# Hand-overs between the sub-layers of a two-layer decoder step: earlier weight splits with a third buffer, moments summed in one accumulator each, and an eviction moved amid a post-norm

## The chip, the core and the metric

The kernel runs on one NeuronCore of one Trainium2 chip. The metric is the device time of one execution in microseconds (us). The engines are named as in the profile: PE is TensorE (PEld its weight loads), DVE is VectorE, ACT is ScalarE, POOL is GpSimd, SP is SyncE, which issues the DMAs. Each engine takes its own instructions in one fixed order.

## What is computed

One inference step of two layers on 512 prompt tokens and 8 x 8 sample tokens, 576 columns in all, model width 1024, in fp32. Each layer is FFN, token mixer, FFN; the mixer of layer 0 is a state-space layer with a gated output (S5 and GLU), that of layer 1 a latent attention (MLA). So there are six sub-layers, n = 0 to 5: FFN, S5, FFN, FFN, MLA, FFN. Every one is wrapped in two norms:

```python
def rms_norm(x, g):
    xf = x.astype(F32)
    y = xf * lax.rsqrt(jnp.mean(xf * xf, axis=-1, keepdims=True) + EPS)
    return (y * g.astype(F32)).astype(x.dtype)

def swiglu(x, w_gate, w_up, w_down):
    return (jax.nn.silu(x @ w_gate) * (x @ w_up)) @ w_down
...
h = swiglu(rms_norm(x, p['norm_pre'][i, 0]), p['ffn_w_gate'][i, 0], p['ffn_w_up'][i, 0], p['ffn_w_down'][i, 0])
x = x + 0.5 * rms_norm(h, p['norm_post'][i, 0])
```

## The kernel before

**Tiling.** Activations lie with the width on the 128 partitions (8 chunks) and the 576 columns in two halves of 288, half 0 and half 1. An fp32 product is made of three matmuls of rounded parts (`mm3`, lines 212 to 215): weight high by activation high, high by low, low by high. So every weight is split after its DMA: ACT copies the high part `whi` and DVE subtracts to the low part `wlo` (`load` in `big_pools`, lines 231 to 241, and `split`, 206 to 210), in pieces of 1024 columns, two for a full unit. The buffers `wlo` and `whi` have a number `nb` of turns: two in sub-layers 0 to 4, three from the output projection of MLA on (`open_w(2)` at line 879, `open_right()` at 1177). `XH` and `XL` (in the trace XHL) are the two parts of the pre-normed activations, `X` the residual, `Y` the output of a sub-layer.

**A hand-over.** The last two output blocks of a sub-layer, m = 6 and 7, run in `tail` (line 287). Their eviction adds to three accumulators over m by `ymom` (line 167): ACC (squares of Y), R (Y times X times gain) and ACQ (squares of Y times gain). For m below 7 the term goes through a buffer `sq` and POOL adds it (in MLA DVE adds ACQ); for m = 7 it stays in a tile of its own (`sqd`, `t`). `mom_a` (line 141) sums all six tiles over the partitions by small matmuls on PE (`sums`, line 100, line L106 of the trace), takes the inverse root of the ACC part on DVE (`rsqrt`, `diag`) and copies the R and ACQ part out (`rs_bc`, line 152). `spread` (line 184, L187) brings the result to all partitions, and `post` (line 274) runs `post1` for the eight chunks k: `t` on DVE (L265), the residual add to X on POOL or DVE (L267), and `xsplit`, the next sub-layer's high part on ACT and low part on DVE (L210). `mom_b` (line 155) forms the statistics of the next pre-norm from the moments, without reading X again.

In program order `tail` runs m = 6 and 7 of half 0, `mom_a` of half 0, m = 6 of half 1, the load and split of the next sub-layer's first weights (W0), all of `post` of half 0, then m = 7 of half 1. `mom_a` and `post` of half 1 are put off (`state["pend"]`) and run inside the next sub-layer's `first_units` (line 316), after its k = 0 and k = 2. `first_units` does two weight units at once: for each k, half 0 of both units, then half 1 unit by unit; the second unit's weights (W1) are loaded just before it (`loads`, line 283).

**What sets the order.** A planner orders the instructions of each engine: it runs the program on its own timing model and gives each engine, whenever that is free, the ready instruction that stands first in the program. Program order is thus a rank and no fixed order. `tc.issue_after(i)` puts what is written inside it behind instruction i on i's engine, and on that engine alone. Between S5 (n = 1) and the FFN before it the tail differs (`nxt == 1`): no split, and half 1's post-norm is spread over S5's own steps.

## Time and profile before

| | us |
|---|---|
| median of 3 runs | 2467.28 (2465.83 to 2472.31) |
| profiled execution | 2468.39 |
| its span, first to last instruction | 2466.6 |
| PE busy in it | 2392.4 (97%) |
| DVE busy | 1301.8 (53%) |
| ACT busy | 888.8 (36%) |
| POOL busy | 565.6 (23%) |

The busy times are unions over the whole span. A matmul's end is modelled, so a busy PE may still run at the lower of its two clocks; PEclk in the page and in the stretches is the granted clock as a share of 2.4 GHz. Idle time of an engine is written in brackets behind the instruction that ended it, with what released that instruction.

### The profile page before, as it was taken

How to read it: one execution, taken by the hardware profiler on the slowest of the kernel's cores; microseconds unless marked ns; L12 is line 12 of the kernel's file. 1: busy time of each engine (PE TensorE's matmuls, PEld its weight loads, DVE VectorE, ACT ScalarE, POOL GpSimd, SP SyncE). 2: the span in 40 equal slices, each digit the busy share in tenths (PEclk: the TensorE clock that was granted, in tenths of full speed). 3: DMA queues.
4: the chain of work that ended last, by engine and by line, in shares of the span. 5: the costliest groups of instructions: out<-in, count | busy, mean ns of one | idle time of the engine just before them, and what ended most of it. 6: DMA issues, size and time to landing. Idle time of an engine off the chain costs nothing. (4 is left out here: it accounts for less than half of the span.)

```text
span 2466.6 us, 44725 instructions
## 1 busy us (share of the span) xinstructions
PE 2392.4 (97%) x17814; PEld 2326.3 (94%) x17814; DVE 1301.8 (53%) x2807; ACT 888.8 (36%) x1864; POOL 565.6 (23%) x820
## 2 busy tenths in 40 slices
PE   7999999799999999999999999999999999999997
PEld 7999999779999999999999999898888899999997
DVE  7565666574564234456323444867777676323334
ACT  4222333374332222333222223424666543223221
POOL 3124455313421001152100115430000042100112
PEclk9999999899999999999999999999999989999999
DMA  3225434462222222122223222346555422222221
GB/s 127 86 76 159 139 127 123 130 178 90 69 86 81 71 98 86 65 82 74 82 73 98 78 79 76 117 123 188 172 166 168 140 78 77 76 87 87 86 71 63
DMA packets 114643, 254.92 MB, mean 103 GB/s; under 512 B 25121, under 2 KB 53538, under 8 KB 114178
## 3 DMA queue, kind: packets, MB, share of 16 engines
q1 hardware_dynamic: 114434, 252.06, 32.3%
q8 instruction: 140, 2.29, 0.4%
q14 instruction: 69, 0.57, 0.1%
HBM read 231.79 MB, written 22.59 MB: 103 GB/s over the span
## 5 line engine op out<-in xcount | busy, mean ns | idle before, releaser
L213 PE MATMUL ps<-XHL,whi 128*128 128x288 f32 x3344 | 997.9, 299 | 17.7 <-ACT whi L208 12.4
L214 PE MATMUL ps<-XHL,whi 128*128 128x288 f32 x3344 | 995.4, 298 | 4.5 <-DVE XHL L210 4.3
L215 PE MATMUL ps<-XHL,wlo 128*128 128x288 f32 x3344 | 988.7, 296 | 2.5 <-DVE wlo L208 2.5
L213 PEld LDWEIGHTS ps<-XHL,whi 128*128 128x128 f32 x3344 | 631.8, 189 | 21.7 <-ACT whi L208 12.8
L214 PEld LDWEIGHTS ps<-XHL,whi 128*128 128x128 f32 x3344 | 633.1, 189 | 8.7 <-DVE XHL L210 7.6
L215 PEld LDWEIGHTS ps<-XHL,wlo 128*128 128x128 f32 x3344 | 633.4, 190 | 3.7 <-DVE wlo L208 3.6
L208 DVE TENSOR_TENSOR wlo<-raw,whi 128x1024 fp32r<-128x1024 f32 (+2 forms) x349 | 410.0, 1199 | 268.1 <-ACT whi L208 267.6
L208 ACT ACTIVATE whi<-raw 128x1024 fp32r<-128x1024 f32 (+2 forms) x349 | 321.6, 946 | 428.8 <-PE ps L214 349.8
L213 PE MATMUL ps<-HH,whi 128*128 128x288 f32 x1408 | 418.8, 297 | 3.9 <-ACT whi L208 3.9
L215 PE MATMUL ps<-HH,wlo 128*128 128x288 f32 x1408 | 417.5, 297 | 1.4 <-DVE wlo L208 1.4
L214 PE MATMUL ps<-HL,whi 128*128 128x288 f32 x1408 | 418.0, 297 | 0.0
L371 POOL TENSOR_TENSOR t<-t,t 128x288 f32<-128x288 f32 x176 | 145.0, 824 | 1086.3 <-DVE t L370 972.4
L213 PEld LDWEIGHTS ps<-HH,whi 128*128 128x128 f32 x1408 | 266.6, 189 | 4.7 <-ACT whi L208 4.4
L215 PEld LDWEIGHTS ps<-HH,wlo 128*128 128x128 f32 x1408 | 266.7, 189 | 2.2 <-DVE wlo L208 2.2
L214 PEld LDWEIGHTS ps<-HL,whi 128*128 128x128 f32 x1408 | 266.8, 189 | 0.2
L370 DVE TENSOR_TENSOR t<-ps,R 128x288 f32<-128x288 f32 x176 | 80.2, 456 | 319.6 <-PE ps L215 319.5
L369 ACT ACTIVATE t<-t 128x288 f32<-128x288 f32 x176 | 77.9, 443 | 332.0 <-DVE t L368 315.8
L208 ACT ACTIVATE HH<-t 128x288 fp32r<-128x288 f32 x176 | 77.0, 438 | 242.4 <-POOL t L371 237.3
L178 POOL TENSOR_TENSOR ACC<-ACC,sq 128x288 f32<-128x288 f32 x72 | 82.4, 1144 | 314.7 <-ACT sq L176 314.7
L208 DVE TENSOR_TENSOR HL<-t,HH 128x288 fp32r<-128x288 f32 x176 | 80.6, 459 | 135.3 <-ACT HH L208 135.0
L368 DVE TENSOR_TENSOR t<-ps,R 128x288 f32<-128x288 f32 x176 | 79.3, 450 | 50.8 <-PE ps L215 50.7
L424 DVE TENSOR_TENSOR Y<-ps,Y 128x288 f32<-128x288 f32 x64 | 29.2, 456 | 122.9 <-PE ps L215 122.9
(362 smaller groups left out, 2766.2 us busy)
## 6 DMA issues: line engine op xcount, KB each, us to landing
raw<-GU SPq DMA_DIRECT2D x176, 512.0 KB, 4.2
pgr<-PG SPq DMA_DIRECT2D x128, 320.0 KB, 3.5
raw<-DN SPq DMA_DIRECT2D x64, 512.0 KB, 3.5
raw<-DN SPq DMA_DIRECT2D x64, 192.0 KB, 3.3
raw<-GLU SPq DMA_DIRECT2D x16, 512.0 KB, 4.5
CAd<-s5w SPq DMA_DIRECT2D x8, 576.0 KB, 6.0
WVd<-s5w SPq DMA_DIRECT2D x8, 512.0 KB, 3.9
wv<-WVd SPq DMA_DIRECT2D x8, 512.0 KB, 5.7
```

The costliest lines, as they stand in the source:

```text
L178: (V if n == 4 and i == 2 else G).tensor_tensor(acc[:, hs(h)], acc[:, hs(h)], dst, op=OP.add)
L208: return A.activation(hi, src, AF.Copy), V.tensor_tensor(lo, src, hi.bitcast(F32), op=OP.subtract)
L213: P.matmul(o, wh, xh, start=st, stop=False)
L214: P.matmul(o, wh, xl, start=False, stop=False)
L215: P.matmul(o, wl, xh, start=False, stop=sp)
L368: V.tensor_tensor(t, pp[0], R[:, hs(h)], op=OP.mult)
L369: A.activation(t, t, AF.Silu)
L370: V.tensor_tensor(u, pp[1], R[:, hs(h)], op=OP.mult)
L371: g = G.tensor_tensor(u, u, t, op=OP.mult)
L424: ins = V.tensor_tensor(y, o, y, op=OP.add)
```

## The change

- `ymom`: for m = 7 the R and ACQ terms are added to their accumulators like the others (except where S5 follows), so these two have one tile each; the ACC term of m = 7 keeps a tile of its own. The ACC add of m = 6 goes from POOL to DVE.
- `mom_a` now sums ACC alone. The sums of R and ACQ are a step of their own, `mom_c`: for half 0 inside the matmuls of m = 6, half 1 (argument `mid`), for half 1 a third entry of `pend`, run after k = 4 of `first_units`.
- `more_w`: one more buffer each for `wlo` and `whi` (`wlx`, `whx`), from the GLU part of S5 to the end of MLA's projections; every third load takes it. Two small constants of MLA (`idb`, `mkb`) lie in the columns 448 to 575 of R.
- W0 is loaded and split after m = 6 of half 0 (after S5: m = 7), and W1 after k = 1 of half 0's `post`.
- Half 0's `post` is cut: k = 0 to 2, then m = 7 of half 1 with its eviction, then k = 3 to 7 (not before S5).
- The third and fourth unit's splits (FFN), or the third's (MLA), stand inside `issue_after` of half 1's `diag`.

```diff
--- before.py
+++ after.py
@@ -44,7 +44,13 @@
             cur["es_w"] = ExitStack()
             cur["load"] = big_pools(cur["es_w"], nb)
 
+        def more_w():
+
+            es = cur["es_w"]
+            cur["more"] = [mkpool(es, nm, 1, side="right", reuse_waits="tile") for nm in ("wlx", "whx")]
+
         def close_w():
+            cur.pop("more", None)
             cur.pop("es_w").close()
 
         def open_right(s5w=False):
@@ -124,7 +130,7 @@
         def diag(y, scale=1.0, tag="a"):
 
             d = smt("rs_d")[:CP]
-            V.scalar_tensor_tensor(d.rearrange("p (j c) -> p j c", j=4),
+            state["dg"] = V.scalar_tensor_tensor(d.rearrange("p (j c) -> p j c", j=4),
                                    ident[:CP, :CP].rearrange("p (o c) -> p o c", o=1).to_broadcast([CP, 4, CP]), 1024.0 * scale,
                                    y.rearrange("p (j o) -> p j o", o=1).to_broadcast([CP, 4, CP]), op0=OP.mult, op1=OP.mult)
             return d
@@ -145,14 +151,17 @@
             V.tensor_scalar(q, src, 1e-6, None, op0=OP.add)
             y = rsqrt(q)
             d = diag(y)
-            bc = None
-            if nxt is not None:
-                pbc = sums([[R[:, hs(h)], SQ[h][1]], [ACQ[:, hs(h)], SQ[h][2]]])
-                bc = cur["sm"].tile([CP, 8], F32, name="rs_bc")
-                V.tensor_copy(bc, pbc)
-            return y, d, bc
-
-        def mom_b(h, y, d_, bc):
+            state["da"] = state["dg"].ins
+            return y, d
+
+        def mom_c(h, SQ):
+
+            pbc = sums([[R[:, hs(h)], *SQ[h][1:2]], [ACQ[:, hs(h)], *SQ[h][2:3]]])
+            bc = cur["sm"].tile([CP, 8], F32, name="rs_bc")
+            V.tensor_copy(bc, pbc)
+            return bc
+
+        def mom_b(h, y, bc):
 
             m = cur["sm"].tile([CP, 4], F32, name="rs_m")
             V.tensor_tensor(m, bc[:, 4:8], y, op=OP.mult)
@@ -169,14 +178,16 @@
             g = GP[:, n, 1, m:m + 1]
             out = []
             for i, acc in enumerate((ACC, R, ACQ)):
-                dst = acc[:, hs(h)] if m == 0 else (smt("t1") if i else sqd.tile([128, H], F32, name="sqd")) if m == 7 else smt("sq")
+                own = m == 7 and (not i or nxt == 1)
+                dst = acc[:, hs(h)] if m == 0 else (smt("t1") if i else sqd.tile([128, H], F32, name="sqd")) if own else smt("sq")
                 if i == 1:
                     V.scalar_tensor_tensor(dst, y, g, X[:, m, hs(h)], op0=OP.mult, op1=OP.mult)
                 else:
                     A.activation(dst, y, AF.Square, scale=g if i else sc)
-                if 0 < m < 7:
-                    (V if n == 4 and i == 2 else G).tensor_tensor(acc[:, hs(h)], acc[:, hs(h)], dst, op=OP.add)
-                out.append(dst)
+                if m and not own:
+                    (V if (n == 4 and i == 2 or m == 6 and i == 0) else G).tensor_tensor(acc[:, hs(h)], acc[:, hs(h)], dst, op=OP.add)
+                if own:
+                    out.append(dst)
                 if nxt is None:
                     break
             return out
@@ -228,9 +239,16 @@
             wlp = mkpool(es, "wlp", nb, side="right", reuse_waits="tile")
             whp = mkpool(es, "whp", nb, side="right", reuse_waits="tile")
 
+            turn = [0]
+
             def load(src, n, mid=None):
-                lo = wlp.tile([128, 2048], F32R, name="wlo")[:, :n]
-                hi = whp.tile([128, 2048], F32R, name="whi")[:, :n]
+                pl, ph = wlp, whp
+                if "more" in cur:
+                    turn[0] += 1
+                    if turn[0] % 3 == 0:
+                        pl, ph = cur["more"]
+                lo = pl.tile([128, 2048], F32R, name="wlo")[:, :n]
+                hi = ph.tile([128, 2048], F32R, name="whi")[:, :n]
                 for c0 in range(0, n, 1024):
                     c = slice(c0, min(n, c0 + 1024))
                     raw = wrp.tile([128, 1024], F32, name="raw")[:, :c.stop - c0]
@@ -281,28 +299,32 @@
             return src.rearrange("p a b c -> p (a b c)")
 
         def loads(n):
-            w = state.pop("W0") if n != subs[0] else cur["load"](first(n, 0), 2048)
-            return [w, cur["load"](first(n, 1), 2048)]
+            return [state.pop("W%d" % u) if n != subs[0] else cur["load"](first(n, u), 2048) for u in range(2)]
 
         def tail(n, blk, mlast, SQ, nxt):
 
             for m in mlast:
                 blk(m, 0)
+                if m == mlast[-1 if n == 1 else 0] and nxt not in (None, 1):
+                    state["W0"] = cur["load"](first(nxt, 0), 2048)
             z = [mom_a(0, SQ, nxt)]
-            blk(mlast[0], 1)
-            if nxt not in (None, 1):
-                state["W0"] = cur["load"](first(nxt, 0), 2048)
-            post(n, 0, spread(z[0][1]), nxt)
-            for m in mlast[1:]:
-                blk(m, 1)
-            state["mom"] = z
+            bc = []
+            if nxt is None:
+                blk(mlast[0], 1)
+            else:
+                blk(mlast[0], 1, lambda: bc.append(mom_c(0, SQ)))
+            rs = spread(z[0][1])
+            state["mom"] = z, bc
             if nxt == 1:
-                s5["D0"] = mom_b(0, *z[0])
+                post(n, 0, rs, nxt)
+                for m in mlast[1:]:
+                    blk(m, 1)
+                s5["D0"] = mom_b(0, z[0][0], bc[0])
 
                 def half1():
                     z.append(mom_a(1, SQ, nxt))
                     spread(z[1][1], ACC[:, hs(1)])
-                    s5["D1"] = mom_b(1, *z[1])
+                    s5["D1"] = mom_b(1, z[1][0], mom_c(1, SQ))
                     end = state["chain"].ins
 
                     def blk1(k):
@@ -311,7 +333,17 @@
                     s5["post"] = blk1
                 state["pend"] = [half1]
                 return
+            for k in range(3):
+                post1(n, 0, rs, nxt, k)
+                if k == 1 and nxt is not None:
+                    state["W1"] = cur["load"](first(nxt, 1), 2048)
+            for m in mlast[1:]:
+                blk(m, 1)
+            for k in range(3, 8):
+                post1(n, 0, rs, nxt, k)
             state["pend"] = [lambda: z.append(mom_a(1, SQ, nxt)), lambda: post(n, 1, spread(z[1][1]), nxt)]
+            if nxt is not None:
+                state["pend"].append(lambda: bc.append(mom_c(1, SQ)))
 
         def first_units(W, evac, K=8):
 
@@ -324,10 +356,10 @@
                 for u in range(2):
                     for g in range(2):
                         mmk(u, pp[u][g], 0, g, k)
-                if k in (0, 2):
+                if k in (0, 2, 4):
                     run_pend(1)
-            z = state["mom"]
-            d0 = diag(mom_b(0, *z[0]))
+            z, bc = state["mom"]
+            d0 = diag(mom_b(0, z[0][0], bc[0]))
             qq = [[], []]
             for u in range(2):
                 for g in range(2):
@@ -339,12 +371,12 @@
                         for v in range(2):
                             evac(v, 0, pp[v])
                     if (u, g) == (0, 1):
-                        d1 = diag(mom_b(1, *z[1]))
+                        d1 = diag(mom_b(1, z[1][0], bc[1]))
             spread(d1, R[:, hs(1)])
             evac(0, 1, qq[0])
             evac(1, 1, qq[1])
 
-        def unit(Wu, h, K=8, G2=2, M=128, xh=None, xl=None):
+        def unit(Wu, h, K=8, G2=2, M=128, xh=None, xl=None, mid=None):
             wh, wl = Wu
             pp = [psum()[:, :H] for g in range(G2)]
             for g in range(G2):
@@ -352,6 +384,8 @@
                     c = slice((g * K + k) * M, (g * K + k) * M + M)
                     mm3(pp[g][:M], wh[:, c], wl[:, c], (XH if xh is None else xh)[:, k, hs(h)],
                         (XL if xl is None else xl)[:, k, hs(h)], k == 0, k == K - 1)
+                if mid and g == 0:
+                    mid()
             return pp
 
 
@@ -407,16 +441,19 @@
                 return W[st]
             for s in range(2):
                 for f in range(0 if s else 2, 11):
-                    Wf = wt((s, 0, f))
+                    with tc.issue_after(state["da"]) if n != subs[0] and (s, f) == (0, 2) else nullcontext():
+                        Wf = wt((s, 0, f))
                     for h in range(2):
                         evac(f, h, unit(Wf, h))
 
-                def down(d, h):
+                def down(d, h, mid=None):
                     wh, wl = wt((s, 1, d))
                     o = psum()[:, :H]
                     for k in range(11):
                         c = slice(k * 128, k * 128 + 128)
                         mm3(o, wh[:, c], wl[:, c], HH[:, k, hs(h)], HL[:, k, hs(h)], k == 0, k == 10)
+                        if mid and k == 7:
+                            mid()
                     y = Y[:, d, hs(h)]
                     if s == 0:
                         tick(A.activation(y, o, AF.Copy))
@@ -897,6 +934,7 @@
                 s_g(k)
             es.close()
             es_c.close()
+            more_w()
             SQ = {}
 
             def gevac(m, h, pp):
@@ -909,10 +947,10 @@
                 gevac(0, h, GL[h])
             W = {}
 
-            def blk(m, h):
+            def blk(m, h, mid=None):
                 if m not in W:
                     W[m] = load(a["GLU"][m].rearrange("p a b c -> p (a b c)"), 2048)
-                gevac(m, h, unit(W[m], h))
+                gevac(m, h, unit(W[m], h, mid=mid))
             for m in range(1, 6):
                 for h in range(2):
                     blk(m, h)
@@ -996,7 +1034,8 @@
                 for x in range(2):
                     V.tensor_tensor(CS[:, x, hs(h)], CS[:, x, hs(h)], RQ[:, hs(h)], op=OP.mult)
             for u in (2, 3):
-                Wu = load(flat(a["WIN"][u]), 2048)
+                with tc.issue_after(state["da"]) if u == 2 else nullcontext():
+                    Wu = load(flat(a["WIN"][u]), 2048)
                 for h in range(2):
                     pp = unit(Wu, h)
                     if h:
@@ -1035,8 +1074,7 @@
             G.memset(Q[0:32, 1:16:2], 0.0)
             KH = qp.tile([128, 2, 512], F32R, name="KH")
             KL = qp.tile([128, 2, 512], F32R, name="KL")
-            idb = qp.tile([128, 128], BF, name="idb")
-            mkb = qp.tile([128, 128], BF, name="mkb")
+            idb, mkb = R[:, 448:512].bitcast(BF), R[:, 512:576].bitcast(BF)
             mnb = qp.tile([128, 8, 64], BF, name="mnb")
 
             CKn = R[:, 0:128].rearrange("p (c j b) -> p c j b", c=2, j=8)
@@ -1201,10 +1239,12 @@
                 if m > 1:
                     SQ[h] = ymom(n, m, h, Y[:, m, hs(h)], nxt)
 
-            def blk(m, h):
+            def blk(m, h, mid=None):
                 o = psum()[:, :H]
                 for k in range(8):
                     mmk(o, m, h, k)
+                    if mid and k == 6:
+                        mid()
                 evac(m, h, o)
             pp = [[psum()[:, :H] for h in range(2)] for m in range(2)]
             for k in range(8):
```

## Rows read from the trace of the kernel before

**Rows 1.** The page of the profile, its parts 1 and 2: busy time, share of the span and instructions of each engine, and the granted clock in 40 equal slices, in tenths of full speed.

```profile
PE 2392.4 (97%) x17814; PEld 2326.3 (94%) x17814; DVE 1301.8 (53%) x2807; ACT 888.8 (36%) x1864; POOL 565.6 (23%) x820
PEclk9999999899999999999999999999999989999999
```

**Rows 2.** The waits of PE over the whole span: who waited, for whom, us in total, times, longest. L213 to L215 are the three matmuls of `mm3`, L187 is `spread`, L106 `sums`, L210 the split of the activations.

```profile
PE ps L213 <- ACT whi L208: 16.3, 5, 8.4
PE ps L187 <- DVE rs_d L127: 10.7, 6, 2.9
PE ps L213 <- ACT XHL L210: 5.2, 10, 0.9
PE ps L214 <- DVE XHL L210: 4.3, 6, 1.3
```

**Rows 3.** Stretches of the four hand-overs n = 1 to 2, 2 to 3, 3 to 4 and 4 to 5, each from the last matmul of m = 7 of half 0 to the last `spread` of the next sub-layer's `first_units`, and as a fifth a stretch of plain FFN. Columns: length, busy us of PE, PEld, DVE, ACT and POOL (instructions), granted clock, DMA share and GB/s.

```profile
652.48:703.71 51.23, 47.80 (x392) 46.17 (x391) 40.88 (x106) 18.93 (x35) 16.85 (x17) 1.00 0.16 51
1090.13:1140.64 50.51, 47.15 (x362) 44.98 (x360) 40.27 (x106) 18.13 (x33) 17.04 (x17) 0.93 0.15 49
1527.19:1578.84 51.65, 47.12 (x363) 44.91 (x361) 41.81 (x109) 18.84 (x35) 20.11 (x21) 0.93 0.31 112
2002.90:2054.55 51.65, 47.84 (x345) 45.80 (x344) 39.80 (x106) 18.98 (x36) 16.83 (x19) 0.87 0.13 40
720.00:1060.00 340.00, 340.00 (x2565) 340.00 (x2565) 124.92 (x189) 95.93 (x164) 41.89 (x50) 1.00 0.25 82
```

**Rows 4.** PE in order of time in the hand-over n = 2 to 3: start, us, line, operation, count, and in brackets the idle time before it and what ended it.

```profile
1090.13 0.62 PE L106 MATMUL ps<-ones,ACC 128*72 128x1 f32 x8
...
1091.65 0.38 PE L213 MATMUL ps<-HH,whi 128*128 128x288 f32 x1
...
1105.83 0.40 PE L214 MATMUL ps<-XHL,whi 128*128 128x288 f32 x1 [1.33 <-DVE XHL L210]
...
1107.70 0.53 PE L213 MATMUL ps<-XHL,whi 128*128 128x288 f32 x2 [0.95 <-ACT XHL L210]
...
1125.89 0.40 PE L213 MATMUL ps<-XHL,whi 128*128 128x288 f32 x1 [0.56 <-ACT XHL L210]
```

**Rows 5.** DVE in order of time in the same hand-over, same columns.

```profile
1094.97 0.16 DVE L152 COPY rs_bc<-ps 72x8 f32<-72x8 f32 x1 [1.09 <-PE ps L106]
...
1099.52 0.46 DVE L424 TENSOR_TENSOR Y<-ps,Y 128x288 f32<-128x288 f32 x1 [1.03 <-PE ps L215]
...
1100.01 0.52 DVE L265 SCALAR_TENSOR_TENSOR t<-Y,GP,ps 128x288 f32<-128x288 f32 x1
...
1100.87 1.22 DVE L208 TENSOR_TENSOR wlo<-raw,whi 128x1024 fp32r<-128x1024 f32 x1
1102.00 1.06 DVE L267 TENSOR_TENSOR X<-X,t 128x288 f32<-128x288 f32 x1
1102.98 1.83 DVE L208 TENSOR_TENSOR wlo<-raw,whi 128x1024 fp32r<-128x1024 f32 x1
1104.73 1.04 DVE L210 SCALAR_TENSOR_TENSOR XHL<-X,GP,XHL 128x288 fp32r<-128x288 f32 x1
...
1107.68 0.52 DVE L210 SCALAR_TENSOR_TENSOR XHL<-X,GP,XHL 128x288 fp32r<-128x288 f32 x1 [0.64 <-ACT XHL L210]
...
1109.10 0.45 DVE L267 TENSOR_TENSOR X<-X,t 128x288 f32<-128x288 f32 x1
...
1113.89 0.45 DVE L424 TENSOR_TENSOR Y<-ps,Y 128x288 f32<-128x288 f32 x1
1114.26 1.21 DVE L208 TENSOR_TENSOR wlo<-raw,whi 128x1024 fp32r<-128x1024 f32 x1
```

**Rows 6.** The six stretches at the lower clock inside those hand-overs; columns as in rows 3, the granted clock stands behind POOL.

```profile
1094.50:1097.90 3.40, 3.40 (x18) 3.40 (x17) 2.52 (x15) 0.00 (x0) 0.00 (x0) 0.50 0.02 5
...
1108.10:1111.50 3.40, 3.37 (x15) 3.24 (x14) 3.40 (x9) 3.40 (x6) 2.21 (x3) 0.50 0.01 2
1531.40:1534.80 3.40, 3.40 (x19) 3.40 (x19) 2.26 (x14) 0.00 (x0) 0.00 (x0) 0.50 0.00 0
1545.00:1548.40 3.40, 3.40 (x15) 3.14 (x15) 3.40 (x9) 3.40 (x6) 2.21 (x3) 0.51 0.10 28
2005.80:2016.00 10.20, 10.00 (x61) 10.00 (x62) 3.22 (x18) 0.00 (x0) 0.14 (x1) 0.50 0.05 20
2026.30:2029.70 3.40, 3.40 (x16) 3.40 (x16) 3.40 (x7) 2.12 (x5) 1.79 (x2) 0.50 0.00 0
```

**Rows 7.** PE in order of time elsewhere: the wait for W1 after S5, the last `spread` in MLA, the start of the sums after MLA, and the first sums of half 1 at the end of the last FFN.

```profile
673.29 0.40 PE L213 MATMUL ps<-XHL,whi 128*128 128x288 f32 x1 [1.64 <-ACT whi L208]
...
1578.84 0.75 PE L187 MATMUL ps<-rs_d,ones 72*128 72x288 f32 x2 [1.33 <-DVE rs_d L127]
...
2004.67 0.68 PE L106 MATMUL ps<-ones,ACC 128*72 128x1 f32 x8 [1.55 <-POOL ACC L178]
2006.00 1.12 PE L106 MATMUL ps<-ones,R 128*72 128x1 f32 x8 [0.65 <-POOL R L178]
...
2451.40 0.62 PE L106 MATMUL ps<-ones,ACC 128*72 128x1 f32 x8
```

**Rows 8.** DVE in order of time at the other two ends of a sub-layer: half 1 of the hand-over from the first FFN to S5, and half 1's last eviction of the last FFN.

```profile
477.82 0.16 DVE L152 COPY rs_bc<-ps 72x8 f32<-72x8 f32 x1 [1.22 <-PE ps L106]
...
2452.31 0.45 DVE L424 TENSOR_TENSOR Y<-ps,Y 128x288 f32<-128x288 f32 x1
```

## The prediction

> **What bounds the kernel now.** I read the page first. PE is busy 97% of the span and the next engine, DVE, 53%; the granted clock is near full in almost every slice [rows 1]. So the end is set by PE, and a change of the other engines can give back only what PE loses: time in which it stands idle, time in which it runs at its lower clock, and matmuls that need not run. The waits of PE tell who keeps it idle: the high part of a weight split (16.3 us), `rs_d`, the inverse root on its way to `spread` (10.7 us), and the splits of the activations (5.2 and 4.3 us) [rows 2]. The longest of the weight waits, 8.4 us, lies at the start of the kernel, which the change leaves alone.
>
> The third view is of stretches. In plain FFN PE is busy 340.00 of 340.00 us at full clock, so there is nothing to gain there. The four hand-overs of 50 to 52 us are different: PE is idle in them for 51.23 - 47.80 = 3.43, 50.51 - 47.15 = 3.36, 51.65 - 47.12 = 4.53 and 51.65 - 47.84 = 3.81 us, together 15.1 us, and in three of them the granted clock is 0.93, 0.93 and 0.87 [rows 3]. Last I read one hand-over in order of time, since the four go alike. DVE meets three things one after the other: the eviction of m = 6 of half 1 at 1099.52, then the two `wlo` pieces of W0 at 1100.87 and 1102.98, and between and behind these the first chunk's residual and split, so that the split that PE needs first begins at 1104.73 and PE has waited 1.33 us. The eviction of m = 7 of half 1, whose matmuls end before PE's wait at 1105.83, comes at 1113.89, after all of half 0's post-norm, and W1's `wlo` after that [rows 4, 5]. Half 1's split is then late too, 0.56 us at 1125.89 [rows 4].
>
> **The change part by part.** The sum is made against the profiled execution, 2468.39 us (span 2466.6, 1.8 us around it); the median of the runs, 2467.28, lies 1.1 us below it.
>
> (a) Fewer sums. Three groups of eight small matmuls take 1091.65 - 1090.13 = 1.52 us of PE at full clock, 0.507 us a group [rows 4]. Each half now has six groups (ACC, R, ACQ and three tiles of m = 7) and will have four. Two groups by two halves by four hand-overs are 16 groups: 8.1 us, all on PE and so on the path. Before S5, and after the last sub-layer, their number stays. The terms that no longer have tiles cost POOL 16 adds; that is (e).
>
> (b) Idle time of PE, 15.1 us. W0's split goes ahead of the tail's end, where DVE and ACT have idle stretches: before m = 6's eviction DVE waits 1.03 us for PE, and before the chain 1.09 us for the sums [rows 5]. That frees the place between `t` and the residual. Now the split of chunk 0 is ready 1104.73 + 1.04 - 1099.52 = 6.3 us after the eviction of m = 6 begins. Without the two pieces (1.22 and 1.83) and with a residual of 0.45 where POOL is quiet, as at 1109.10, in place of 1.06, it would be 2.6 us: 6.3 - 3.05 - 0.61. PE's 33 matmuls of m = 7 of half 1 lie between and take 33 x 340/2565 = 4.4 us [rows 3]. So the wait for chunk 0 goes with some 1.8 us to spare, and the ACC add that comes to DVE in that place (0.45, the same tile shape) fits in. W1 was the 1.64 us wait after S5 [rows 7]; its split now comes after chunk 1. There it is late next: two pieces of 1.22 us stand in DVE's order ahead of chunks 2 and on, and PE has only two chunks of work in hand. Its price is between nothing (the planner puts them into gaps) and the 3.05 us that W0's pieces take there now. I take 1.0 us per hand-over, nearer to nothing, since the chunks' work for PE (12 matmuls, 1.6 us each) is longer than DVE's for a chunk (0.52 + 0.52 and, for two in eight, 0.45: some 1.2 us). Half 1's eviction comes up to 8 us earlier, so its 0.56 us goes, and I count half of the last `spread`'s 1.33 us in MLA as gone. After MLA PE waits 1.55 us for POOL's ACC add and 0.65 us for R [rows 7]; the first goes to DVE and the second gets the matmuls of m = 6 as cover; I leave 0.7 us of that. Of 15.1 us there stay 4.0 + 0.7 + 0.7, and 1.9 of short gaps: gain 7.8 us, bounds 2 and 15.
>
> (c) Clock. The six stretches at 1.2 GHz add up to 27.2 us [rows 6]; PE is busy in nearly all of it and does half as much, so they cost 13.5 us. Each comes either right behind the sums with their idle time (1094.50, 1531.40, 2005.80) or behind the idle time at the start of the next units (1108.10, 1545.00, 2026.30). Both causes shrink and neither goes. I let the 10.2 us stretch fall to 3.4 (3.4 us gained) and one of the others go (1.7): 5.1 us, bounds 0 and 13.5.
>
> (d) The two other ends. Before S5, DVE stands 1.22 us at the copy of the R and ACQ sums with the chain behind it [rows 8], at one of the points where PE waits for `rs_d`; the copy now follows the chain, and I take 0.8 of it. At the end the last eviction begins at 2452.31 behind half 0's post-norm [rows 8], while PE is past its last matmul at 2451.40 [rows 7], so it gains 0.9 us at most, and the rest of the post-norm fits under the chain that follows: 0.7 us. Together 1.5 us, bounds 0 and 2.1.
>
> (e) What is added. POOL gets 16 adds (R and ACQ, m = 7; ACQ after MLA goes to DVE) of about 0.8 us. POOL itself is idle for most of a hand-over: 16.85 us busy of 51.23 [rows 3]. But DVE's split of a chunk took 1.04 us at 1104.73 beside POOL's adds and 0.52 us at 1107.68 without [rows 5]: 0.52 us per meeting. Eight of the adds, those of half 1, fall into the time in which PE lives on DVE's chunks; if a quarter of these meets a step that PE waits for, 1.1 us is lost; bounds 0 and 8.3 (all 16). The moved issues of W0 and W1 pass only weight loads on SP's queue, and the `issue_after` holds back the low splits of the next units, which PE needs some 25 us later. The third buffer and the constants in R cost nothing in time as long as their former users are done, which they are: R's last reader before is a projection step. If that cover were gone, it would be a split late by one unit, 1.22 us.
>
> The Trainium skill, on the page "SBUF — State Buffer", section "SBUF: two separate sides", speaks against more adds on POOL: VectorE and GpSimd share one pair of ports, and an operation of VectorE with two inputs in SBUF and one of GpSimd exclude each other for a whole instruction. By that rule every meeting costs DVE the rest of POOL's add, and all 16 adds would take the gain of (e)'s upper bound, some 8 us, off the sum. The trace agrees in kind, with 1.83 for 1.22 us and 1.04 for 0.52 us.
>
> Sum: 8.1 + 7.8 + 5.1 + 1.5 - 1.1 = 21.4 us, 2447.0 for a profiled execution, 2446 for the median.
>
> **The rivals.** *W1's split starves PE.* DVE takes instructions in one order. If the planner puts W1's two pieces ahead of chunk 2 and POOL's adds stretch them to 1.83 us, PE waits 3.0 us instead of 1.0 in each hand-over (8 us), and the idle time keeps the clock stretches (5.1 us): 2468.39 - 21.4 + 13.1 = 2460.1, 2459 for the median. For it: exactly this happened with W0's pieces. Against: ACT and DVE are idle under m = 6 and 7, and W1's buffer is free once m = 6 is over.
>
> *The order stays as it was.* The planner goes by its own times; if it still evicts m = 7 of half 1 after the post-norm, only the sums (8.1 us), the W1 wait (1.6) and part of (d) remain: some 11 us, 2456. For it: it let that eviction lie for 8 us. Against: what made it lie is the rank, and the rank changes.
>
> *Slower.* The low splits of the third and fourth unit, four pieces of 1.22 us, are held behind half 1's `diag` but not behind half 1's post-norm. If DVE takes them right after `diag`, half 1's first chunk is 4.9 us later. It decides at the slack that half 1 has: with its eviction some 8 us earlier, 4.9 us is hidden; without that, PE waits 4.9 us in four hand-overs, 19.6 us, and after each the clock falls once more, 4 x 1.7 = 6.8 us. Against that only the sums stand: 26.4 - 8.1 = 18 us slower, 2485. Against it: the post-norm stands ahead of these splits in the program.
>
> **How the numbers follow.** Forecast 0.60, W1 starves PE 0.17, order as before 0.14, slower 0.09. A difference of 0.3%, 7.4 us, is about what a measurement of this kernel can tell from no change; that is 2459.9 and 2474.7. The forecast's own bounds are 8.1 + 15 + 13.5 + 2 = 38.6 us (2429) and 8.1 + 2 + 0 + 0 - 8.3 = 2 us (2465), ends that need every term at once; I take 2434 to 2456 as its own range. The two middle rivals reach 2462. The range is 2434 to 2462; outside stay the slower case, and some 0.1 of the others. Faster by over 0.3%: the forecast but for 0.03, half of W1's case and most of the third, 0.77; within 0.3%: 0.14; slower: 0.09.
>
> **What would show it.** In the hand-overs: 32 small matmuls per half instead of 48; each stretch shorter by some 4 to 6 us and PE's idle time in it 1 to 2.5 us; W0's `wlo` before the sums; the copy `rs_bc` behind the chain; the eviction of m = 7 of half 1 right behind its matmuls and within half 0's post-norm; no wait for the XHL of chunk 0 of either half. Fewer than six stretches at the lower clock. It is wrong if DVE has `wlo` pieces in front of the chunk that PE waits for, if the lower clock lasts as long as before, or if time is lost outside the hand-overs, in the units that now load one step earlier.

## The result and the profile after

| | before | after |
|---|---|---|
| median | 2469.8 us (2465.83 to 2473.18, 4 runs) | 2449.04 us (2447.3 to 2452.29, 4 runs) |
| ratio to before | | 0.9923, 95% interval 0.9905 to 0.9941 |
| profiled execution, span | 2466.6 us | 2445.5 us |

The kernel became 0.8% faster, 21.1 us in the span; the forecast was 2446 within 2434 to 2462. Line numbers below are those of the changed kernel: L224 to L226 are `mm3`, L198 is `spread`, L112 `sums`, L221 the split of activations, L219 the split of weights.

First part 1 of the page, in answer to [rows 1]: the share of PE is the same, and its 128 matmuls fewer are the 16 groups of sums.

```profile
PE 2375.5 (97%) x17686; PEld 2311.2 (95%) x17686; DVE 1310.7 (54%) x2821; ACT 889.4 (36%) x1864; POOL 570.9 (23%) x822
```

Then the stretches, as in [rows 3]: the four hand-overs, and behind them MLA from the last `spread` of its first units to the hand-over that follows.

```profile
651.60:700.80 49.20, 46.18 (x360) 45.40 (x359) 39.76 (x107) 19.01 (x35) 19.43 (x20) 0.97 0.16 49
1087.30:1132.50 45.20, 42.83 (x330) 41.29 (x327) 39.64 (x107) 18.41 (x33) 20.19 (x20) 0.96 0.17 56
1519.10:1565.90 46.80, 42.10 (x330) 39.80 (x328) 42.21 (x109) 17.93 (x34) 24.62 (x24) 1.00 0.33 118
1987.10:2033.70 46.60, 40.78 (x313) 39.21 (x312) 40.43 (x110) 18.90 (x36) 17.55 (x19) 0.96 0.18 59
...
1565.90:1987.10 421.20, 412.04 (x2668) 376.76 (x2668) 299.30 (x761) 238.39 (x636) 70.16 (x65) 0.98 0.47 151
```

The hand-overs took 205.04 us in [rows 3] and take 187.80. PE's idle time in them did not shrink: 3.02 + 2.37 + 4.70 + 5.82 = 15.9 us against 15.1. What shrank is its busy time, 189.91 to 171.89 us. 8.1 us of that are the sums (32 or 33 matmuls fewer in each stretch, at the 0.507 us a group of [rows 4]). Most of the rest is the clock: length times what is missing of the granted clock makes 13.9 us in [rows 3] and 1.5 + 1.8 + 0 + 1.9 = 5.2 here. DVE's busy time is the same, 162.0 us against 162.8; it now fills 86% of the hand-overs, where it filled 79%.

The stretches at the lower clock, in answer to [rows 6]; the third lies behind the end of its hand-over and costs 3.3 us in MLA, so the clock's net gain is 8.7 - 3.3 = 5.4 us. In another execution of the same kernel (e5 below) that third stretch is only 3.4 us long.

```profile
681.70:685.10 3.40, 3.40 (x16) 3.40 (x15) 2.99 (x7) 1.92 (x4) 2.57 (x3) 0.51 0.40 146
1115.10:1118.50 3.40, 3.40 (x17) 3.40 (x16) 2.99 (x7) 1.92 (x4) 2.66 (x3) 0.51 0.46 159
1565.70:1572.50 6.80, 6.62 (x25) 6.33 (x26) 4.76 (x8) 4.07 (x9) 2.62 (x2) 0.50 0.14 45
2012.80:2016.20 3.40, 3.40 (x17) 3.40 (x16) 2.98 (x7) 1.93 (x4) 2.49 (x3) 0.51 0.39 141
```

MLA's part took 1578.84 to 2002.90, 424.06 us, in the kernel before, and takes 421.20. Its row of before, in the same view, shows PE idle for 14.2 us; in the last row of the stretches above it is 9.2:

```profile
1578.84:2002.90 424.06, 409.87 (x2668) 374.38 (x2668) 300.98 (x762) 239.55 (x637) 70.36 (x65) 0.98 0.48 152
```

The waits of PE over the whole span tell who took over, against [rows 2]: `rs_d` from 10.7 to 16.9 us, and longer ones for the sums' inputs (`sqd` 3.7 us before, now 5.7; ACC 1.6 us before, for POOL's add, now 2.4 for DVE's), while the waits for activation splits are down to 2.5 and 0.4 us and of those for `whi` none lies in a hand-over.

```profile
PE ps L198 <- DVE rs_d L133: 16.9, 10, 2.9
PE ps L224 <- ACT whi L219: 14.7, 4, 8.4
...
PE ps L112 <- ACT sqd L186: 5.7, 3, 2.8
...
PE ps L225 <- DVE XHL L221: 2.5, 4, 0.7
PE ps L112 <- DVE ACC L188: 2.4, 1, 2.4
```

PE in order of time in the hand-over n = 2 to 3, as in [rows 4], and behind it the largest wait of each of the other three:

```profile
1099.65 0.40 PE L225 MATMUL ps<-XHL,whi 128*128 128x288 f32 x1 [0.59 <-DVE XHL L221]
...
1101.60 0.40 PE L226 MATMUL ps<-XHL,wlo 128*128 128x288 f32 x1 [0.36 <-DVE wlo L219]
1101.84 0.62 PE L112 MATMUL ps<-ones,ACC 128*72 128x1 f32 x8
...
1103.80 0.68 PE L112 MATMUL ps<-ones,sqd 128*72 128x1 f32 x8
...
1112.66 0.75 PE L198 MATMUL ps<-rs_d,ones 72*128 72x288 f32 x2 [1.35 <-DVE rs_d L133]
...
671.87 0.68 PE L112 MATMUL ps<-ones,sqd 128*72 128x1 f32 x8 [1.77 <-ACT sqd L186]
...
1565.88 1.33 PE L198 MATMUL ps<-rs_d,ones 72*128 72x288 f32 x2 [2.63 <-DVE rs_d L133]
...
1989.68 0.68 PE L112 MATMUL ps<-ones,ACC 128*72 128x1 f32 x8 [2.44 <-DVE ACC L188]
```

In n = 2 to 3 the 1.33 us for the first chunk is 0.59, with 0.36 us for a `wlo` piece behind it; half 1's 0.56 has gone, and 1.35 stands at half 1's `spread`, where there was nothing. DVE in the same stretch shows why, beside [rows 5]:

```profile
1097.22 1.40 DVE L219 TENSOR_TENSOR wlo<-raw,whi 128x1024 fp32r<-128x1024 f32 x1
1098.55 1.05 DVE L221 SCALAR_TENSOR_TENSOR XHL<-X,GP,XHL 128x288 fp32r<-128x288 f32 x1
...
1101.88 0.45 DVE L461 TENSOR_TENSOR Y<-ps,Y 128x288 f32<-128x288 f32 x1
...
1107.33 0.15 DVE L151 TENSOR_SCALAR rs_a<-ps 72x4 f32<-72x4 f32 x1
1107.40 1.50 DVE L221 SCALAR_TENSOR_TENSOR XHL<-X,GP,XHL 128x288 fp32r<-128x288 f32 x2
1109.18 0.70 DVE L221 SCALAR_TENSOR_TENSOR XHL<-X,GP,XHL 128x288 fp32r<-128x288 f32 x1 [0.29 <-ACT XHL L221]
1110.17 0.52 DVE L221 SCALAR_TENSOR_TENSOR XHL<-X,GP,XHL 128x288 fp32r<-128x288 f32 x1 [0.29 <-ACT XHL L221]
1110.61 0.16 DVE L119 TENSOR_SCALAR rs_ya<-rs_a 72x4 int32<-72x4 int32 x1
1110.68 0.15 DVE L121 SCALAR_TENSOR_TENSOR rs_tb<-rs_yb 72x4 f32<-72x4 f32 x1
...
1112.14 0.46 DVE L133 SCALAR_TENSOR_TENSOR rs_d<-ident,rs_ya 72x288 f32<-72x288 f32 x1
...
1112.89 1.21 DVE L219 TENSOR_TENSOR wlo<-raw,whi 128x1024 fp32r<-128x1024 f32 x1
1114.02 0.93 DVE L283 SCALAR_TENSOR_TENSOR t<-Y,GP,ps 128x288 f32<-128x288 f32 x2
```

A `wlo` piece of W1 stands in front of the first chunk's split (W0's two are done before the hand-over begins), and PE waits for both. The eviction of m = 7 of half 1 is where the prediction wanted it (1101.88, before 1113.89). But half 1's chain, whose sums PE ends at about 1104.5, waits: its first step is at 1107.33, the second at 1110.61, with four splits of half 0's last chunks between, and then it goes in turns with half 0's other chain (`rs_tb`). Behind `rs_d` a `wlo` piece of a later unit stands ahead of half 1's post-norm.

### The profile page after: what moved, and what is told of

Its sections match the earlier page's. It is cut to its first block, busy times and chain, and to the rows that moved or that the text cites. A ratio compares the mean times of both kernels' runs of the same rounds, so it can differ in the third digit from the quotient of the medians.

```text
span 2445.5 us, 44507 instructions
## 1 busy us (share of the span) xinstructions
PE 2375.5 (97%) x17686; PEld 2311.2 (95%) x17686; DVE 1310.7 (54%) x2821; ACT 889.4 (36%) x1864; POOL 570.9 (23%) x822
## 5 line engine op out<-in xcount | busy, mean ns | idle before, releaser
L224 PE MATMUL ps<-XHL,whi 128*128 128x288 f32 x3344 | 997.8, 299 | 11.2 <-ACT whi L219 10.8
L226 PE MATMUL ps<-XHL,wlo 128*128 128x288 f32 x3344 | 988.1, 296 | 2.9 <-DVE wlo L219 2.9
L224 PEld LDWEIGHTS ps<-XHL,whi 128*128 128x128 f32 x3344 | 631.7, 189 | 12.7 <-ACT whi L219 10.9
L226 PEld LDWEIGHTS ps<-XHL,wlo 128*128 128x128 f32 x3344 | 633.0, 189 | 4.3 <-DVE wlo L219 4.2
L219 DVE TENSOR_TENSOR wlo<-raw,whi 128x1024 fp32r<-128x1024 f32 (+2 forms) x349 | 410.4, 1198 | 265.1 <-ACT whi L219 264.1
L219 ACT ACTIVATE whi<-raw 128x1024 fp32r<-128x1024 f32 (+2 forms) x349 | 322.0, 946 | 420.0 <-PE ps L225 357.7
L224 PE MATMUL ps<-HH,whi 128*128 128x288 f32 x1408 | 417.5, 297 | 3.9 <-ACT whi L219 3.9
L226 PE MATMUL ps<-HH,wlo 128*128 128x288 f32 x1408 | 416.1, 296 | 1.4 <-DVE wlo L219 1.4
L224 PEld LDWEIGHTS ps<-HH,whi 128*128 128x128 f32 x1408 | 265.0, 188 | 4.7 <-ACT whi L219 4.4
L226 PEld LDWEIGHTS ps<-HH,wlo 128*128 128x128 f32 x1408 | 264.9, 188 | 2.2 <-DVE wlo L219 2.2
L219 ACT ACTIVATE HH<-t 128x288 fp32r<-128x288 f32 x176 | 77.1, 439 | 250.4 <-POOL t L405 244.3
L219 DVE TENSOR_TENSOR HL<-t,HH 128x288 fp32r<-128x288 f32 x176 | 81.1, 461 | 134.6 <-ACT HH L219 134.4
L188 POOL TENSOR_TENSOR ACC<-ACC,sq 128x288 f32<-128x288 f32 x60 | 68.8, 1147 | 233.2 <-ACT sq L186 233.2
```

What stands on the lines that cost most here:

```text
L188: (V if (n == 4 and i == 2 or m == 6 and i == 0) else G).tensor_tensor(acc[:, hs(h)], acc[:, hs(h)], dst, op=OP.add)
L219: return A.activation(hi, src, AF.Copy), V.tensor_tensor(lo, src, hi.bitcast(F32), op=OP.subtract)
L224: P.matmul(o, wh, xh, start=st, stop=False)
L226: P.matmul(o, wl, xh, start=False, stop=sp)
```

## The experiments

Two theories came first, a third after the second group of runs. Theory 1: the gain is PE's work that is gone and the clock that came with it; idle time only moved. Theory 2: it is stalls taken out by splits, buffer and cut. Theory 3: the edits took what PE lost until DVE's own work in a hand-over was the limit, so single edits stand in for one another and only DVE's load or order moves the end. Each group of four ran on one chip beside the kernel before; gains are taken from the ratios to it.

**First group: undo or do one part.** The medians of the kernel before were 2471.17 us (2462.62 to 2474.49).

```
e1_six_sums
-                own = m == 7 and (not i or nxt == 1)
+                own = m == 7
e2_two_bufs
-            more_w()
e3_post_whole
-            for k in range(3):
+            for k in range(8):
                 post1(n, 0, rs, nxt, k)
...
-            for k in range(3, 8):
-                post1(n, 0, rs, nxt, k)
e4_sums_alone (the kernel before, with)
+                own = m == 7 and (not i or nxt == 1)
...
+            pbc = sums([[R[:, hs(h)], *SQ[h][1:2]], [ACQ[:, hs(h)], *SQ[h][2:3]]])
...
+                blk(mlast[0], 1, lambda: bc.append(mom_c(0, SQ)))
...
+                state["pend"].append(lambda: bc.append(mom_c(1, SQ)))
```

> The changed kernel with the moments of m = 7 in tiles of their own again in every hand-over, so that each half's second and third moments are again summed over two tiles instead of one; split order, third buffer and cut post-norm stay. Theory 1 (the gain is mostly TensorE work that is gone: 16 groups of small matmuls, some 8 us, and the time at the lower clock that came with them, some 8 us; idle time only changed its place): 8 to 14 us slower than the changed kernel, that is 7 to 13 us faster than the kernel before. Theory 2 (the gain is stalls taken out by the splits, the third buffer and the cut; the sums were hidden in waits anyway): 0 to 4 us slower than the changed kernel.

Measured: 2454.38 us (2451.16 to 2458.48), ratio 0.9932, interval 0.9916 to 0.9948: 16.8 us faster than before. The changed kernel stands at 0.9923 and, measured again below, 0.9909, that is 19 and 22.5 us faster, so the six sums cost 2 to 6 us, less than theory 1 said and nearer to theory 2. The sum over its four hand-overs (columns as above):

```profile
sum 199.20, PE 191.14 PEld 185.97 DVE 160.80 ACT 74.27 POOL 67.58; mean PE 47.78 PEld 46.49 DVE 40.20 ACT 18.57 POOL 16.89
```

PE is idle for 199.20 - 191.14 = 8.1 us only, which looks like the gain that (b) forecast. But the granted clock of the four was 0.90, 0.93, 0.90 and 0.89, so length times what is missing is 18.9 us, against 13.9 in [rows 3]: idle time had become slow work. Idle time and missing clock together were 15.1 + 13.9 = 29.0 us before and are 27.0 here and 15.9 + 5.2 = 21.1 in the changed kernel. This execution is the slowest of its six, so it overstates the case.

> The changed kernel without the third buffer of split weights, all else kept. Theory 1 (fewer sums and the clock carry the gain): within 4 us of the changed kernel. Theory 2 (stalls on split weights carried it): 8 us or more slower than the changed kernel, with waits for whi and wlo back in the hand-overs. The projections of the MLA stage, 2.8 us shorter in the changed kernel, should go back to their old length under both if the third buffer is what shortened them.

Measured: 2454.08 us (2450.53 to 2460.54), 0.9938 (0.9919 to 0.9957): 15.3 us faster than before, 4 to 7 slower than the changed kernel, between the theories. The profiled execution is longer in two places. The hand-overs take 193.60 us against 187.80, at clocks of 0.90, 1.00, 0.96 and 0.96, and of theory 2's signs a wait for `whi` of 1.37 us after S5 is back, at 671.65 (1.64 us before the change):

```profile
sum 193.60, PE 178.48 PEld 169.15 DVE 163.13 ACT 75.06 POOL 77.08; mean PE 44.62 PEld 42.29 DVE 40.78 ACT 18.77 POOL 19.27
```

In MLA, from its last `spread` (at 1612.28 in the changed kernel) to the hand-over, it takes 378.10 us, against 374.80 in the changed kernel and 380.70 before, and PE's wait for `wku` is back, as are two in attention (1.14 us, and 0.66 us for `pgk` at 1695.00). In order: the stretch of e2, its waits (with e2's line numbers), and the stretch of the changed kernel.

```profile
1616.80:1994.90 378.10, 367.36 (x2352) 332.57 (x2352) 267.21 (x673) 220.55 (x597) 51.66 (x52) 0.99 0.51 160
```

```profile
1664.13 0.50 PE L226 MATMUL ps<-CKH,wku 128*128 128x512 f32 x1 [1.41 <-DVE wku L219]
...
1690.53 0.66 PE L1416 MATMUL ps<-ident,Pm 128*128 128x128 f32 x4 [1.14 <-ACT Pm L1297]
```

```profile
1612.30:1987.10 374.80, 367.73 (x2352) 333.69 (x2352) 263.65 (x671) 219.37 (x595) 50.83 (x52) 0.98 0.49 159
```

So the third buffer also works in MLA, where the prediction had not looked, and W1's wait after S5 goes by the buffer: e2 has the earlier split without it.

> The changed kernel with all eight post-norm steps of half 0 before half 1's last block, as in the kernel before; sums, splits and third buffer stay. Theory 1: within 3 us of the changed kernel either way, since the wait of the last evictions comes back (about 1 us in each of four hand-overs) and the wait for half 1's spread (0.7 to 1.35 us in each) goes, its chain being no longer behind five XH/XL splits on VectorE. Theory 2 (the cut is where the idle time went out): 5 us or more slower, with 1 to 2 us more of idle TensorE in each hand-over.

Measured: 2450.92 us (2447.05 to 2455.55), 0.9921 (0.9902 to 0.9939): as the changed kernel. The cut of the post-norm by itself brings nothing that can be measured, as theory 1 said.

> The kernel before with only the moments changed: one accumulator each, the second and third moments' sums moved to their own place, the add of m = 6 on VectorE; weights' splits, two buffers and post-norm as before. Theory 1: 12 to 16 us faster than the kernel before (ratio 0.9935 to 0.995), the hand-overs' clock up as in the changed kernel. Theory 2: 3 to 7 us faster, idle TensorE time in the hand-overs grown by what the sums lost.

Measured: 2458.45 us (2453.75 to 2460.53), 0.9948 (0.993 to 0.9965): 12.8 us faster, theory 1's number. But everything except the sums (e1) gave 16.8. Together that would be 29.6 us, and the changed kernel has 19 to 22.5; the difference is at the edge of what the intervals allow. Either part alone takes much of the same gain. In e4 PE's idle time in the hand-overs is 194.00 - 178.53 = 15.5 us, at clocks of 1.00, 0.96, 0.96 and 0.86. So neither sign came whole: the clock did not rise as in the changed kernel, and the idle time did not grow:

```profile
sum 194.00, PE 178.53 PEld 170.32 DVE 169.03 ACT 75.34 POOL 77.79; mean PE 44.63 PEld 42.58 DVE 42.26 ACT 18.83 POOL 19.45
```

**Second group: the wait that is left.** Kernel before 2468.55 us (2463.47 to 2473.25).

```
e6_late_spread
-                if k in (0, 2, 4):
+                if k in (0, 3, 4):
e7_momc_first
-                state["pend"].append(lambda: bc.append(mom_c(1, SQ)))
+                state["pend"].insert(1, lambda: bc.append(mom_c(1, SQ)))
e8_late_both: both
```

> The changed kernel itself once more, beside the three variants that follow, so that they are compared with it on one chip. 0.9915 to 0.993 of the kernel before, whatever the theory.

Measured: 2445.3 us (2441.16 to 2449.26), 0.9909 (0.9893 to 0.9925).

> The changed kernel with half 1's spread after the fourth chunk of the next first units instead of after the third, so that TensorE has one more chunk (some 1.6 us) of work before it needs rs_d. Theory 1 (the idle time that is left waits for half 1's chain, which stands on VectorE behind the splits of half 0's chunks 3 to 7): the waits of 0.7 to 1.4 us for rs_d at that spread go in all four hand-overs, 2 to 4 us in all, and come back at most in part as waits for half 1's first chunk: 1 to 4 us faster than the changed kernel. Theory 2 (half 1's split chunks are the limit, and the chain is not): as much is lost at the first matmul of half 1 as is gained at the spread, 0 to 2 us slower.

Measured: 2445.42 us (2442.44 to 2448.49), 0.9913 (0.9897 to 0.9928). It decides little: in three hand-overs the planner, which sets the order, left `spread` in its place on PE, and the waits are those of the changed kernel. In n = 2 to 3 the 1.3 us wait at half 1's `spread` went and 1.24 us came at the last one instead; the time is the same.

> The changed kernel with half 1's second and third moments summed and copied before its post-norm instead of after it. Theory 1: the waits of the last spread for the chain behind that copy (1.25 us after MLA, 2.63 us in it) go, 2 to 3 us in all, but the sums come before the last adds of VectorE and GpSimd may be done and TensorE can wait there 0 to 1 us in each hand-over: 0 to 3 us faster. Theory 2: VectorE has no room there, the copy delays half 1's first chunk by as much: 0 to 3 us slower.

Measured: 2445.28 us (2443.95 to 2453.28), 0.9916 (0.9901 to 0.9932): no difference. Yet the order did change: the sums of the second and third moments now fill the wait for `rs_d` at half 1's `spread`, which is gone or 0.4 us in all four hand-overs. Two new waits took its place at half 1's first chunk, after S5 and after MLA:

```profile
690.85 0.54 PE L224 MATMUL ps<-XHL,whi 128*128 128x288 f32 x2 [1.51 <-ACT XHL L221]
```

```profile
2017.11 0.40 PE L224 MATMUL ps<-XHL,whi 128*128 128x288 f32 x1 [2.00 <-ACT XHL L221]
```

> Both of the two runs before: sums of the second and third moments after the fourth chunk, spread and post-norm after the fifth. Theory 1: 2 to 5 us faster than the changed kernel, half 1's first chunk being just in time. Theory 2: half 1's first chunk is late by 1 to 3 us in each hand-over, 3 to 8 us slower.

Measured: 2446.72 us (2443.53 to 2448.19), 0.9913 (0.9899 to 0.9928): no difference either. Three orders of PE's work (e5, e7, e8), one time: this is what led to theory 3, since the time did not change with the result that PE happened to wait for.

**Third group: VectorE's load.** Kernel before 2468.51 us (2462.05 to 2474.77).

```
e9_twice_t (in post1)
-            V.scalar_tensor_tensor(t, ...
+            for _ in range(2 if h and nxt not in (None, 1) else 1): V.scalar_tensor_tensor(t, ...
e10_later_issue (in post1, with xsplit returning its split)
-                xsplit(nxt, h, k)
+                state.update(da=xsplit(nxt, h, k)[1].ins if h else xsplit(nxt, h, k) and state["da"])
e11_later_momc: e10 with e7's line
e12_no_issue
-    with tc.issue_after(state["da"]) if ... else nullcontext():
+    with nullcontext():
```

> The changed kernel with half 1's eight products t of the post-norm each computed twice into the same place: eight more VectorE operations of some 0.47 us, 3.7 us in each of four hand-overs, 15 us in all, on VectorE alone. Theory 3 (since the change VectorE's own order of work sets the length of a hand-over: it is busy 162.0 of 187.8 us there against 162.8 of 205.0 before, and its last steps run without a gap): 10 to 15 us slower than the changed kernel, each hand-over longer by 2.5 to 3.7 us. Rival (the waits that are left are latencies between engines, and VectorE has 12% of slack in these stretches): 0 to 5 us slower.

Measured: 2466.98 us (2465.12 to 2469.22), 0.9997 (0.9987 to 1.0006): 22 us slower than the changed kernel beside its second measurement, 18 beside its first. The whole gain of the change is gone, for 15 us of VectorE work alone; that is more than the 10 to 15 us of theory 3. The sum over the four hand-overs:

```profile
sum 202.70, PE 176.49 PEld 166.67 DVE 177.41 ACT 76.71 POOL 72.77; mean PE 44.12 PEld 41.67 DVE 44.35 ACT 19.18 POOL 18.19
```

DVE is busy 177.4 - 162.0 = 15.4 us more and the stretches are 202.7 - 187.8 = 14.9 us longer: theory 3's mechanism, and not the rival with its 12% of slack. The rest of the 20.5 us between the two profiled spans lies outside: the FFN stretches behind the first two hand-overs are 1.6 and 2.8 us longer, their first 13.9 and 15.8 us at a granted clock of 0.88 and 0.80 against 1.00 in the changed kernel, and 1.2 us in what came before the first hand-over and in MLA. The wait comes out at the last `spread`, in the hand-over n = 2 to 3:

```profile
1144.24 1.33 PE L198 MATMUL ps<-rs_d,ones 72*128 72x288 f32 x2 [3.91 <-DVE rs_d L133]
```

> The changed kernel with the third unit's weight loads held behind the last split of half 1 instead of behind its diagonal, so that the low split of 1.2 us that VectorE has between half 1's rs_d and the first step of its post-norm comes after that post-norm. Theory 3: half 1's chunks and the evictions that follow come up to 1.2 us earlier in four hand-overs, 2 to 4 us faster than the changed kernel. Rival (half 1 is not late, so VectorE's piece costs nothing there): within 1 us of the changed kernel. If the weights are then late for the third unit, a wait for wlo or whi shows up and it is 1 to 4 us slower.

Measured: 2442.44 us (2440.9 to 2443.46), 0.9898 (0.9883 to 0.9912), the fastest of all and 25 us below the kernel before; against the changed kernel 2.7 us (0.9909) to 6 us (0.9923), with intervals that overlap. Theory 3's 2 to 4 us fit, but a gain is not shown. On DVE the post-norm now follows `rs_d` without the `wlo` piece:

```profile
1115.24 0.45 DVE L133 SCALAR_TENSOR_TENSOR rs_d<-ident,rs_yb 72x288 f32<-72x288 f32 x1
1116.17 0.94 DVE L283 SCALAR_TENSOR_TENSOR t<-Y,GP,ps 128x288 f32<-128x288 f32 x2 [0.48 <-PE ps L198]
```

```profile
sum 184.40, PE 170.44 PEld 163.92 DVE 155.80 ACT 72.19 POOL 83.44; mean PE 42.61 PEld 40.98 DVE 38.95 ACT 18.05 POOL 20.86
```

6.2 us of DVE's work moved out of the hand-overs, and they are 3.4 us shorter. That is not theory 3 stretch by stretch: the last one is 3.6 us shorter, while n = 2 to 3 has 2.1 us less of DVE's work and is 0.9 us longer.

> The run before together with half 1's second and third moments ahead of its post-norm. Theory 3: the waits for half 1's first chunk that the earlier moments brought (1.51 us after S5, 2.00 us after MLA) shrink by the 1.2 us of the low split that no longer stands ahead, so that the two together are 3 to 6 us faster than the changed kernel. Rival: no difference that can be measured, as with the earlier moments alone.

Measured: 2443.28 us (2440.45 to 2446.94), 0.9905 (0.9889 to 0.9921): not better than e10 alone, and 1 to 4 us faster than the changed kernel. The wait after S5 shrank to 1.09 us, the one after MLA stayed at 1.95. A miss for theory 3's 3 to 6 us.

> The changed kernel without holding back the loads of the next units behind half 1's diagonal. Theory 3: more low splits of 1.2 us come ahead of half 1's chain or post-norm on VectorE, one to three in each hand-over, 3 to 10 us slower than the changed kernel. Rival: the order of VectorE hardly changes and the time stays within 1.5 us.

Measured: 2444.69 us (2443.34 to 2447.38), 0.9907 (0.9892 to 0.9921): as the changed kernel; theory 3 had 3 to 10 us slower. In n = 2 to 3 two low splits go ahead of half 1's `rs_d` instead of one behind it, but none is left between it and the post-norm, and over the four hand-overs DVE's busy time grows by 1.7 us only:

```profile
sum 190.40, PE 176.03 PEld 168.46 DVE 163.72 ACT 75.58 POOL 75.91; mean PE 44.01 PEld 42.12 DVE 40.93 ACT 18.90 POOL 18.98
```

Holding the loads behind `diag`, as the change does, brings nothing that these runs can measure. Whether all of DVE's work in a hand-over counts, or only what stands in half 1's chain and post-norm, no run separates: e9's added work stands in that post-norm.

## Why the prediction was right, and where it was not

The total was near, 21.1 us of span for a forecast of 21.4 (the median came out 3 us above it), but by luck: two errors nearly cancelled.

(a) Fewer sums, 8.1 us: the 16 groups are gone from PE. (c) The clock, 5.1 us: 5.4 measured in this execution, one stretch having moved behind its hand-over.

(b) is the step that failed: "Of 15.1 us there stay 4.0 + 0.7 + 0.7, and 1.9 of short gaps: gain 7.8 us". 15.9 us of idle time stayed. W1's pieces, its largest term, were priced high: the waits for `whi` and for half 1's first chunk went, and W1 costs 0.59 + 0.36 us in n = 2 to 3, as much in n = 3 to 4, and nothing that shows in the other two, 1.9 us of the 4.0. But a piece stands ahead of the first chunk's split, not behind the second's, and so do the ACC add (0.45) and the second chunk's `t` (0.50); the residual took 1.07 us beside POOL, where the prediction had 0.45. So that split ends 5.5 us after the eviction of m = 6 begins (at 1094.08), and not 2.6.

The step failed in the rest: 12.2 us stand where it left 0.7 + 0.7. Two waits that it named as gone or halved grew: the last `spread` in MLA from 1.33 to 2.63 us, the sums after MLA from 1.55 to 2.44, with the ACC add on DVE instead of POOL. Three are new: half 1's `spread` in all four hand-overs (1.24, 1.35, 0.66 and 0.84 us), `sqd` after S5 (1.77) and a `spread` after MLA (1.25). The error was to add (a) and (b) as if each were free of the other. Before, half 1's sums of the second and third moments stood between its first sums and its `spread` and covered the chain; now PE stands at `spread` instead. e7 puts them back into that wait and loses no time by it, and e1 and e4 each give most of the gain alone.

The step looked for what is late next only among W1's pieces, and not at DVE's total, which the change hardly lowers: 40.88, 40.27, 41.81 and 39.80 us in each hand-over [rows 3]. DVE's idle time in the four together fell from 42.3 us to 25.8, and is 25.3 in e9 and 25.0 in e4: from there on, more work on DVE made longer hand-overs, 14.9 us for 15.4 in e9. It is no fixed floor (28.6 us in e10; 38.4 in e1, at its lower clock), and that DVE is what holds e7's and e8's orders to one time is argued, not shown.

Net of the stretch that moved into MLA, the hand-overs gave 17.2 - 3.3 = 13.9 us where (a), (b), (c) and (e) made 19.9, so 6.0 us are missing.

Unpredicted: MLA, 424.06 - 421.20 = 2.9 us shorter although it took over 3.3 us of lower clock, so some 6 us; e5's execution, with 1.6 us of lower clock there, took 418.00. "The third buffer and the constants in R cost nothing in time" was true and too little: e2 shows that the buffer ends the 1.41 us wait for `wku` and keeps attention's start from waiting, 3.3 us of MLA, beside what it brings in the hand-overs. The rest stays without the buffer: the same stretch took 421.50 us in e2 and 422.60 in e4, each in a single execution; what gives it is open.

(d), 1.5 us: not shown before S5. The copy does follow the chain now, but PE's wait for `rs_d` there grew from 2.04 to 2.65 us, and the sums of the first hand-over start at 651.6 (before 652.48) in one execution and at 654.27 in e5's. At the end 411.8 against 412.05 us, 0.25 of 0.7. (e), 1.1 us lost: not seen in DVE's sum. Its large steps took the same time with the added adds as without; the changed kernel first, then the kernel before, in the hand-over n = 2 to 3 by line (count, busy us, mean ns):

```profile
L221 DVE SCALAR_TENSOR_TENSOR XHL<-X,GP,XHL 128x288 fp32r<-128x288 f32 x16 | 10.1, 661 | 2.1 <-ACT XHL L221 2.0
L283 DVE SCALAR_TENSOR_TENSOR t<-Y,GP,ps 128x288 f32<-128x288 f32 x16 | 7.6, 504 | 0.0
L219 DVE TENSOR_TENSOR wlo<-raw,whi 128x1024 fp32r<-128x1024 f32 x6 | 7.5, 1247 | 0.0
L285 DVE TENSOR_TENSOR X<-X,t 128x288 f32<-128x288 f32 x4 | 3.0, 757 | 0.0
```

```profile
L210 DVE SCALAR_TENSOR_TENSOR XHL<-X,GP,XHL 128x288 fp32r<-128x288 f32 x16 | 10.2, 681 | 1.5 <-ACT XHL L210 1.5
L208 DVE TENSOR_TENSOR wlo<-raw,whi 128x1024 fp32r<-128x1024 f32 x6 | 7.9, 1318 | 0.0
L265 DVE SCALAR_TENSOR_TENSOR t<-Y,GP,ps 128x288 f32<-128x288 f32 x16 | 7.5, 505 | 0.6 <-PE ps L187 0.6
L267 DVE TENSOR_TENSOR X<-X,t 128x288 f32<-128x288 f32 x4 | 2.4, 601 | 0.0
```

28.2 against 28.0 us. By the Trainium skill's rule of the shared port ("SBUF — State Buffer", section "SBUF: two separate sides") an operation of DVE with two inputs in SBUF and one of POOL shut each other out; with it the prediction estimated some 8 us if all 16 adds met one. The rule may hold for each meeting (the first chunk's 1.05 us beside POOL fits it); these sums show no more time lost to meetings than before.

The rivals. W1's split did get ahead of the chunk that PE waits for, as the first rival had it, but at 0.95 us and not 3.0; and the order did change. The slower one was in part there: not four low splits but one, 1.21 us at 1112.89, came between half 1's `diag` and its post-norm. What it costs is not shown: e10, which takes it away, has a median 3 to 6 us lower by intervals that overlap, and its stretch n = 2 to 3 is no shorter. Of the signs named ahead, the orders came as written, but for W1's piece, and PE's idle time did not: 2.4 to 5.8 us a hand-over instead of 1 to 2.5.

Open: how much of e1's short idle time was the lower clock of that one execution; what gives the rest of MLA's gain, and why e12 costs nothing that its 2.6 us of longer hand-overs would lead to expect; differences of that size are within the spread of one kernel's runs (8 us in e5).

## What to carry to other kernels

Before gains in one stretch are added up, write the busy time of every engine in that stretch beside its length: where the second engine is nearly as busy as the stretch is long, it may cap the sum of all edits, and one edit may only replace another. Test this by giving that engine more work of a known size; if the stretch grows by the same amount, that engine stands in the path there, and the next thing to try is to take work from it, or to move work past the stretch's end. A buffer that is added for one place frees waits wherever its pool is used, so read the waits of every stage that loads through it.

## What was not expected of the hardware

The order of work does not settle the lower clock alone. Two profiled executions of one kernel, the changed one and e5, have the same hand-overs to 0.3 us (187.80 and 187.53), at the same clocks, but behind n = 3 to 4 the clock stays low for 6.8 us in one and 3.4 in the other, and the runs of that kernel lie between 2441.2 and 2452.3 us in two measurements. The times go with the mean granted clock of a run: among the 17 of the kernel before in the third group the slowest, 2474.77 us, had 0.979 and the fastest, 2462.05, had 0.986. In e7 three of the four hand-overs ran at a granted clock of 1.00, with as much idle time in the four as in the changed kernel (16.4 us against 15.9), and its median is the same.
